# Value projections computed by rows of time, another order of the projection pairs, and a reworked first pass in an f32 hybrid encoder block

## The chip, the cores and the metric

The kernel runs on one core of one Trainium2 chip. Its engines each follow their own queue of instructions: TensorE (PE in the profile; PEld is its weight load) multiplies matrices, VectorE (DVE), ScalarE (ACT) and GpSimd (POOL) work on tiles in on-chip memory, and SyncE (SP) issues the transfers between device memory and on-chip memory. Matmuls write to PSUM, all other tiles are in SBUF. The metric is the device time of one execution in microseconds.

## The reference, cut to what matters

One encoder block on `x` of 2048 rows of time by 1024 columns, all in float32. One wide projection feeds everything else:

```python
h = rms_norm(x, norm_pre_g)
proj = jnp.einsum('bsd,de->bse', h, w_in)
u_a, z_a, q, k, v, o, z_b, gates, g_a, g_b = jnp.split(proj, split_points, axis=-1)   # 1024 columns each, gates 16
# branch A: centred window means of u_a, mixed per group, times silu(z_a)
# branch B: q, k = silu(centred depthwise conv); 4 heads of 256, chunks of 128 rows, both directions:
kw = kc * jnp.exp(w_end - m_chunk[..., None])[..., None]
c_chunk = jnp.einsum('bhcld,bhcle->bhcde', kw, vc)          # added to a running state, chunk after chunk
num = jnp.einsum('bhcls,bhcsd->bhcld', scores, vc) + inter_scale[..., None] * num_inter
# hb = sum of the directions, normalised per head; y_b = hb * sigmoid(o) * silu(z_b)
merged = jax.nn.sigmoid(g_a + b_merge[0]) * (y_a @ w_proj_pool) + jax.nn.sigmoid(g_b + b_merge[1]) * (y_b @ w_proj_mlstm)
return x + rms_norm(merged @ w_out, norm_post_g)
```

The values `v` are used with time on the rows of a matmul's operands (`kw` transposed times `vc`), while q and k are first convolved along time.

## The kernel before

**Arithmetic.** Every f32 product is made of three matmuls in a reduced-precision form of f32 (fp32r in the rows): each operand is split into an upper part (a rounded copy) and a lower part (what the copy lost), and upper x upper, upper x lower and lower x upper are added in PSUM. A split is one copy, mostly on ScalarE (L98), and one subtraction on VectorE or GpSimd (L102). Names that end in `h` and `l` are the two parts.

**Projections.** The first two thirds of the program are the projections. They run over two halves of the sequence of 1024 rows each, and in each half over 36 *pairs* of column blocks of the weights (128 columns each). `in_pairs` lists them: the merge gates `ga` and `gb` of head 0 first, then *heavy* pairs (q, k, u), each followed by some *light* ones (v, z, o with zb, and other gates), then three gate pairs. For each half, one level of the Strassen-Winograd scheme is used: the 1024 rows are two blocks of 512, the 1024 inputs two of 512, the pair's two column blocks are the third factor. `operands` makes the seven left operands from the normalised, transposed input (A11, A12, A22, S1 to S4), `prep_w` the seven right ones from the pair's weights (B11, B21, B22, T1 to T4; tiles named `wB` and `wT`). The seven products go into three accumulators `bankA`, `bankB`, `bankC`, each with two buffers in PSUM (`strassen`). One product is 4 slices x 3 terms = 12 matmuls of 512 columns, with a 128x128 weight block as the stationary operand and 512 rows of time as the moving one. So results have output columns on partitions and time along the free axis. The first two pairs of a half, `ga` and `gb` of head 0, are done without Strassen (`quarters`, L500 to L502), as their operands are ready sooner. In the first half the split weights are kept in device memory (`keep_w`) and half of them are read back in the second (`again_w`).

**Value pairs.** `pair_v` collects the four result quadrants in two tiles `raw` (L685: VectorE adds the last term while it reads PSUM). Then TensorE turns them, 128x128 at a time, against an identity matrix (`vtr`, L744), eight transposes for each block of 512 rows; the turned values are split to `vnh` and `vnl` and stored. These tiles carry two more columns, ones and zeros, which VectorE sets by memset as soon as the tile is free (L737). There are four value pairs (one per head) and two halves.

**First pass.** In the first half, before the loop of pairs, `operands` fetches the transposed input (`xT`), sums its squares (`ssqp`, L258), spreads the row factors by a matmul with the identity (`rbp`, L183), scales, and makes the combinations; two products `busy` (L281), whose result nothing reads, stand between these. `combos` splits S1 and S3 with their lower parts on GpSimd and S2 with its lower part on VectorE. The last input tiles live in rooms that the weight tiles (`wc`, 10 buffers) take over later. `gates` makes the 16 gate pre-activations beside the first pairs and copies them out of PSUM as `gsb` (L671). `fold` (L373, L379) multiplies the pooled branch's mixing and projection matrices together, piecewise between pairs at the places listed in `FOLDS`.

**Recurrence.** After the projections, `mlstm` walks over heads and chunks. Backward first: `back1` turns a chunk's keys (`kt`, L1311, two transposes of 128x128 each) and weighs them (`keys`), `back2` multiplies them with the values (`update`: `cu`, L1040 to L1042, two tiles of 128x258) and adds to the running state `cb` on VectorE (L1256), 15 states per head and direction. For head 0 backward, `keys` has a branch of its own: ScalarE writes the weighed key to a tile from the pool `w1`, VectorE copies the upper part (L1268), GpSimd subtracts. For all others ScalarE writes the upper part at once and VectorE makes the lower one (L1245). After the recurrence come the two merged branches (`branch_a`, `branch_b`) and the output projection. In the second half of the projections, weights that these later stages need are split ahead (`split_ahead`, 16 steps, one per pair from pair 12 on, `PRE`).

**What sets the order.** The program is written as generators of small steps; a tile scheduler puts each engine's instructions in order by the order of writing, by priorities (`tc.high_priority`: the weights of the next pair are prepared ahead) and by ties (`tc.issue_after(x)`: not before x in the order). All transfers of tiles are issued by SyncE. The weights of pair 2 are tied behind the last scaled input (`self.scaled[8]`), those of pair 3 are not tied.

The main loop after the two first pairs does, for each pair: prepare the weights, first product steps, the rest of the pair before, own middle steps:

```python
this, self.read_banks = work(i, W), []
next(this)
...
next(this)
run(rest)
...
next(this)
rest = this
```

The functions follow as the kernel before has them.

## Time and profile before

| | |
|---|---|
| runs of the kernel before | 2341.11, 2343.8, 2347.96 us; median 2343.8 us |
| profiled execution | 2344.1 us, span from first to last instruction 2342.3 us |
| mean granted TensorE clock | 0.993 |
| TensorE busy | 2285.9 us, 98% of the span, 11545 matmul records |
| VectorE, ScalarE, GpSimd busy | 1412.6 us (60%), 885.8 us (38%), 1184.2 us (51%) |
| transfers | 564.43 MB, mean 241 GB/s |

All rows are of one profiled execution. A group row names line, engine, operation and tiles (output <- inputs), the tile's partitions x elements and the count, then busy time, the mean of one, and the idle time just before such instructions with what ended most of it. A row of a timeline begins with the time from the span's start, then the time that the row covers, engine, line and what it is; `x4` says that four like ones are in the row, and brackets at the end give a wait and what ended it. A row of stretches gives, for each window, its length and then the busy time of TensorE, of its weight load, of VectorE, ScalarE and GpSimd, the granted clock, the busy share of the DMA engines and GB/s. Matmuls overlap in the pipeline, so a matmul's own duration (0.39 us for 512 columns) is longer than the distance from one start to the next.

### The profile page before, as it was taken

The numbers are of one execution on the slowest core, as the hardware profiler recorded it, in microseconds if no ns is written. First come the engines' busy times: TensorE is split into PE (matmuls) and PEld (weight loads), VectorE is DVE, ScalarE is ACT, GpSimd is POOL, SyncE is SP. The second block draws the span as 40 slices with busy tenths as digits, with TensorE's granted clock in tenths as the row PEclk, the third lists the DMA queues.
The fourth block names the chain that finished last, engine by engine and source line by source line (L and its number), as shares of the span: only waits on it lengthen the run. The fifth ranks groups of instructions, "written<-read, shape, count | busy, mean of one in ns | idle before, by whom it ended". The sixth has DMA issues, their size and how long they took to land. (4 is left out here: it accounts for less than half of the span.)

```text
span 2342.3 us, 32965 instructions
## 1 busy us (share of the span) xinstructions
PE 2285.9 (98%) x11545; PEld 1938.1 (83%) x11545; DVE 1412.6 (60%) x2379; ACT 885.8 (38%) x1796; POOL 1184.2 (51%) x917
## 2 busy tenths in 40 slices
PE   7899999999999999999999999899999999999998
PEld 5788888888888788888878788699998888999886
DVE  6665656768765555546656565388887453454365
ACT  5334333333343423323333233467766221111342
POOL 4755545666664533356564555245556341233574
PEclk9999999999999999999999999899999999999999
DMA  5567766766685366788888787767767696677863
GB/s 211 188 237 271 259 222 223 265 234 219 222 296 206 110 203 212 228 297 279 295 298 287 265 299 270 258 193 246 238 190 243 219 321 227 214 277 256 329 207 126
DMA packets 233270, 564.43 MB, mean 241 GB/s; under 512 B 23568, under 2 KB 70800, under 8 KB 233104
## 3 DMA queue, kind: packets, MB, share of 16 engines
q1 hardware_dynamic: 233104, 562.33, 69.7%
q8 instruction: 91, 1.49, 0.3%
q14 instruction: 75, 0.61, 0.1%
HBM read 340.46 MB, written 221.77 MB: 240 GB/s over the span
## 5 line engine op out<-in xcount | busy, mean ns | idle before, releaser
L102 POOL TENSOR_TENSOR wB<-wraw,wB 128x512 fp32r<-128x512 f32 x220 | 333.1, 1518 | 293.3 <-ACT wB L98 232.7
L98 ACT ACTIVATE wB<-wraw 128x512 fp32r<-128x512 f32 x224 | 139.3, 626 | 268.7 <-PE bankB L112 121.9
L102 POOL TENSOR_TENSOR wT<-wt,wT 128x512 fp32r<-128x512 f32 x102 | 148.5, 1459 | 128.2 <-ACT wT L98 105.5
L718 DVE SCALAR_TENSOR_TENSOR acc<-raw,conv_w,acc 128x1026 f32<-128x1026 f32 (+1 forms) x96 | 151.2, 1587 | 10.5 <-ACT acc L713 9.7
L1040 PE MATMUL pb<-oxs,w_proj_mlstm 128*128 128x256 f32 x512 | 143.9, 281 | 0.7 <-DVE sga L1206 0.4
L1042 PE MATMUL pb<-oxs,w_proj_mlstm 128*128 128x256 f32 x512 | 143.9, 281 | 0.0
L1041 PE MATMUL pb<-oxs,w_proj_mlstm 128*128 128x256 f32 x512 | 143.8, 281 | 0.0
L98 ACT ACTIVATE wT<-wt 128x512 fp32r<-128x512 f32 x136 | 85.3, 629 | 153.5 <-PE bankB L112 60.4
L1385 POOL TENSOR_TENSOR qs<-q,isc 128x256 f32<-128x256 f32 x120 | 90.0, 754 | 93.1 <-PE num L1401 59.9
L110 PE MATMUL bankB<-S3h,wT 128*128 128x512 f32 x272 | 106.2, 390 | 3.6 <-DVE u L469 3.6
L110 PE MATMUL bankB<-A22h,wT 128*128 128x512 f32 x272 | 106.1, 390 | 2.1 <-DVE u L474 2.1
L110 PE MATMUL bankA<-A12h,wB 128*128 128x512 f32 x272 | 108.0, 397 | 0.0
L110 PE MATMUL bankC<-S4h,wB 128*128 128x512 f32 x272 | 106.2, 391 | 1.2 <-DVE raw L685 1.2
L112 PE MATMUL bankA<-A11h,wB 128*128 128x512 f32 x272 | 106.0, 390 | 1.3 <-POOL wB L102 1.3
L1025 POOL TENSOR_TENSOR nm<-nm,mask 128x256 f32<-128x256 f32 x64 | 60.4, 955 | 91.4 <-DMA nm<-negM 74.2
L111 PE MATMUL bankB<-S2l,wT 128*128 128x512 f32 x272 | 106.5, 392 | 0.0
L110 PE MATMUL bankC<-S1h,wT 128*128 128x512 f32 x272 | 106.4, 391 | 0.0
L111 PE MATMUL bankC<-S4l,wB 128*128 128x512 f32 x272 | 106.4, 391 | 0.0
L112 PE MATMUL bankA<-A12h,wB 128*128 128x512 f32 x272 | 106.2, 391 | 0.0
L110 PE MATMUL bankA<-A11h,wB 128*128 128x512 f32 x272 | 106.2, 390 | 0.0
L111 PE MATMUL bankA<-A12l,wB 128*128 128x512 f32 x272 | 106.1, 390 | 0.0
L112 PE MATMUL bankC<-S4h,wB 128*128 128x512 f32 x272 | 106.1, 390 | 0.0
(417 smaller groups left out, 7097.3 us busy)
## 6 DMA issues: line engine op xcount, KB each, us to landing
wt<-wT SPq DMA_DIRECT2D x136, 512.0 KB, 4.4
wT<-wt SPq DMA_DIRECT2D x136, 512.0 KB, 6.0
wraw<-in_w_in SPq DMA_DIRECT2D x98, 512.0 KB, 5.2
vh<-vnh SPq DMA_DIRECT2D x16, 516.0 KB, 4.4
vl<-vnl SPq DMA_DIRECT2D x16, 516.0 KB, 5.7
v<-vh SPq DMA_DIRECT2D x16, 516.0 KB, 8.8
v<-vl SPq DMA_DIRECT2D x16, 516.0 KB, 8.5
xT<-in_xT SPq DMA_DIRECT2D x16, 512.0 KB, 6.5
```

The lines of the kernel that those rows point to most:

```text
L98: self.upper = nc.scalar.activation(hi, x, AF.Copy)
L102: return eng.tensor_tensor(lo, x, hi.bitcast(F32), op=ALU.subtract)
L110: nc.tensor.matmul(ps, wh, xh, start=start and kt == 0, stop=False, skip_group_check=True)
L111: nc.tensor.matmul(ps, wh, xl, start=False, stop=False, skip_group_check=True)
L112: end = nc.tensor.matmul(ps, wl, xh, start=False, stop=stop and kt == 3, skip_group_check=True)
L718: nc.vector.scalar_tensor_tensor(acc[:, :n], raw[:, tap : tap + n], self.cw[:, ct, tap : tap + 1], acc[:, :n], op0=ALU.mult, op1=ALU.add,)
L1025: nc.gpsimd.tensor_tensor(t[:, d, :, :], t[:, d, :, :], mask[:, d, None, :].to_broadcast([P, 2, P]), op=ALU.add)
L1040: nc.tensor.matmul(ps, wh, xh, start=i == 0, stop=False)
L1041: nc.tensor.matmul(ps, wh, xl, start=False, stop=False)
L1042: nc.tensor.matmul(ps, wl, xh, start=False, stop=i == n)
L1385: nc.gpsimd.tensor_tensor(qs[d], q[:, :, ck], isc[:, d, j % 2, None, :].to_broadcast([P, 2, P]), op=ALU.mult)
```

## The change

**Values by rows.** `pair_v` no longer collects and turns. Two value pairs are done together by a new function `by_rows`: the stationary operand is now 128 rows of time of an A or S operand, the moving one 256 columns of the weights of the two pairs together, so that the results have time on partitions. The weights of the value pairs are laid out for it (`columns` in `layouts`, `in_pairs`): two neighbouring value pairs now hold the columns of two heads (0 and 2, then 1 and 3), the one pair for the first half of each input block's slices, the other for the second. A product is 48 matmuls of 256 columns for the two pairs (2 pairs' input slices x 2 x 4 time blocks x 3 terms); there are 14 such products for each half. Each accumulator's two buffers belong to the same two pairs. Splits read the results directly (those of the first quadrant from PSUM, the others from SBUF), the memset of the extra columns is tied behind the split, and the first of the two pairs only runs what is left of the pair before.

**Order of the pairs.** The first two value pairs follow q of head 0, the other two follow q of head 1 (loop places 3, 4 and 8, 9); the other light pairs are spread anew. The 16 steps of `split_ahead` stand at the places listed in `PRE` in place of 12 to 27, and one place of `FOLDS` changes from 9 to 10.

**First pass.** In the first half S1's lower parts are made on VectorE. The tile of input slices 2 and 3 of the second block is now in a `raw` room, that of slices 4 and 5 in a `wc` room. The first `busy` product is tied behind the last `ssqp`, and two stand behind `rbp` where there was one. The weights of pair 3 are tied behind the last copy of the first pairs' evacuation (`self.evac`) and behind `gsb` (`self.gated`).

**Keys.** The branch of `keys` for head 0 backward is gone; these keys go the way of all others, with its two buffers.

```diff
-PRE = 12
-FOLDS = (2, 5, 7, 9, 12, 14, 16, 18)
+PRE = (4, 5, 7, 9, 10, 16, 17, 19, 20, 22, 24, 25, 27, 29, 32, 33)
+FOLDS = (2, 5, 7, 10, 12, 14, 16, 18)
...
+        c = base["v"] + h // 2 * DH
+        one["v", h] = ("v", (h // 2, h % 2), c, c + 2 * DH)
...
-    light = [("v", 0), ("o", 0), ("o", 1), ("v", 1), ("o", 2), ("v", 2), ("o", 3), ("o", 4), ("z", 0), ("o", 5)]
-    light += [("z", 1), ("v", 3), ("o", 6), ("z", 2), ("o", 7)]
+    light = [[("v", 0), ("v", 1)], [("o", 0)], [("v", 2), ("v", 3)], [("o", 1)], [("o", 2)], [("o", 3), ("z", 0)]]
+    light += [[("o", 4), ("z", 1)], [("o", 5)], [("o", 6), ("z", 2)], [("o", 7)], [edge[5], ("z", 3)], edge[6:]]
...
-        self.put(H, "S1", j, s1, "act", "pool")
+        self.put(H, "S1", j, s1, "act", le)
...
-        for b, q, where in ((0, 0, "raw"), (0, 2, "acc"), (0, 1, "acc"), (0, 3, "acc"), (1, 0, "raw"), (1, 2, "raw"), (1, 1, wc), (1, 3, wc)):
+        for b, q, where in ((0, 0, "raw"), (0, 2, "acc"), (0, 1, "acc"), (0, 3, "acc"), (1, 0, "raw"), (1, 1, "raw"), (1, 2, wc), (1, 3, wc)):
...
-            busy(X[7][0][:, :P], X[7][0])
+            with tc.issue_after(done.ins):
+                busy(X[7][0][:, :P], X[7][0])
...
-            busy(self.rstd[:, :1].to_broadcast([P, P]), X[7][0])
+            for _ in range(2):
+                busy(self.rstd[:, :1].to_broadcast([P, P]), X[7][0])
...
-        ends = [self.combos(H, j, X[j][0], X[4 + j][0], X[j][1], X[4 + j][1]) for j in range(4)]
+        ends = [self.combos(H, j, X[j][0], X[4 + j][0], X[j][1], X[4 + j][1], ("dve", "pool")[half]) for j in range(4)]
...
-                            with tc.issue_after(self.scaled[8].ins) if i == 2 else ExitStack():
+                            ties = [self.scaled[8]] if i == 2 else [self.evac, self.gated] if i == 3 else []
+                            with ExitStack() as behind:
+                                for t in ties:
+                                    behind.enter_context(tc.issue_after(t.ins))
                                 self.prep_w(W, load(i), wc, wt)
...
-                    if half == 1 and PRE <= i < PRE + 2 * KT:
+                    if half == 1 and i in PRE:
...
+                    if self.pairs[i][0] == "v":
+
+                        if self.pairs[i][1][1] == 0:
+                            first = W
+                            run(rest)
+                        else:
+                            run(work(i, (first, W)))
+                        rest = iter(())
+                        if half == 0 and i + 1 in FOLDS:
+                            next(fold)
+                        continue
...
-                        nc.tensor.transpose(ps[:, c, i * P : (i + 1) * P], t[i][:, tt : tt + P], self.ident)
-                cc = slice(c2 * 2, c2 * 2 + 2)
-                self.split(hi[:, cc, :DH], lo[:, cc, :DH], ps, "act", "dve")
...
+    def by_rows(self, H, W, psum, pool, out):
...
+        def prod(k, h, w, start):
+            for t in range(2):
+                wh, wl = (x.rearrange("p (k a) n -> p k (a n)", k=2) for x in W[t][w])
+                for tt in range(4):
+                    ps = bank[k, tt // 2][:, tt % 2, :]
+                    for j in range(2):
+                        hh, hl = (x[:, 2 * t + j, tt * P : (tt + 1) * P] for x in H[h])
+                        opens, end = start and t + j + tt % 2 == 0, t + j == 2
+
+                        with self.tc.issue_after(opened.ins) if start and not opens else ExitStack():
+                            one = nc.tensor.matmul(ps, hh, wh[:, j], start=opens, stop=False, skip_group_check=True)
+                        if opens:
+                            opened = one
+                        nc.tensor.matmul(ps, hh, wl[:, j], start=False, stop=False, skip_group_check=True)
+                        self.third = nc.tensor.matmul(ps, hl, wh[:, j], start=False, stop=end, skip_group_check=True)
...
+        prod("A", "A11", "B11", True)
+        p1 = copy("A")
+        prod("B", "S2", "T2", True)
+        u2 = plus("B", p1)
+        yield
+        prod("C", "S1", "T1", True)
+        prod("B", "S3", "T3", False)
+        u3 = plus("B", p1)
+        yield
+        give(3, "C", u3)
+        prod("A", "A12", "B21", False)
+        give(0, "A", None)
+        yield
+        prod("B", "A22", "T4", False)
+        give(2, "B", p1)
+        prod("C", "S4", "B22", False)
+        give(1, "C", u2)
...
-                if d == 1 and h == 0:
-
-                    kw = self.w1.tile([P, 2, 512], F32, tag="w", name=self.nm("kw"))[:, 0, :DH]
-                    k = self.w1.tile([P, 2, 512], F32R, tag="w", name=self.nm("k"))
-                    out = k[:, 0, :DH], k[:, 1, :DH]
-                    up = nc.scalar.activation(kw, kn[h, c // 4][:, c % 4, :], AF.Copy, scale=col["w"][:, ix(d, h, c)])
-                    nc.vector.tensor_copy(out[0], kw)
-                    nc.gpsimd.tensor_tensor(out[1], kw, out[0].bitcast(F32), op=ALU.subtract)
...
                 out = split2(io, [P, DH], f"k{d}", bufs=KB)
-                weigh(out, kn[h, c // 4][:, c % 4, :], col["w"][:, ix(d, h, c)])
+                up = weigh(out, kn[h, c // 4][:, c % 4, :], col["w"][:, ix(d, h, c)])
```

Three places where the order of an engine's instructions changes. Line numbers of the change are those of the changed file.

**ScalarE at the end of the first block.** `sg` is the sigmoid of the first two pairs' merge gates, `gsb` the copy of the gate pre-activations, `wB` and `wT` are upper parts of weights: the first two of pair 2, the others of pair 3. Before:

```order
L98 ACTIVATE wT_94_850<-wt_848 128x512
L98 ACTIVATE wB_95_853<-wraw_825 128x512
L841 ACTIVATE sg_781<-bankC_636,b_merge 128x512
L98 ACTIVATE wB_110_956<-wraw_952 128x512
L841 ACTIVATE sg_784<-bankC_637,b_merge 128x512
L98 ACTIVATE wT_113_963<-wt_961 128x512
L841 ACTIVATE sg_793<-bankA_644,b_merge 128x512
L98 ACTIVATE wT_114_966<-wt_959 128x512
L841 ACTIVATE sg_796<-bankB_645,b_merge 128x512
L671 ACTIVATE gsb_801<-gps_688 32x512
L98 ACTIVATE wT_116_971<-wt_969 128x512
```

After:

```order
L101 ACTIVATE wT_95_852<-wt_850 128x512
L101 ACTIVATE wB_96_855<-wraw_827 128x512
L930 ACTIVATE sg_783<-bankC_638,b_merge 128x512
L930 ACTIVATE sg_786<-bankC_639,b_merge 128x512
L930 ACTIVATE sg_795<-bankA_646,b_merge 128x512
L930 ACTIVATE sg_798<-bankB_647,b_merge 128x512
L692 ACTIVATE gsb_803<-gps_690 32x512
L101 ACTIVATE wB_111_958<-wraw_954 128x512
L101 ACTIVATE wT_114_965<-wt_963 128x512
L101 ACTIVATE wT_115_968<-wt_961 128x512
L101 ACTIVATE wT_117_973<-wt_971 128x512
```

The three splits for pair 3 that stood between the sigmoids now stand behind `gsb`.

**TensorE in the first value work of the first half.** `bankB` is the accumulator of the second of the seven products' chains, `vtr` the PSUM tile that takes the transposes, `raw` the collected results. Before:

```order
L112 MATMUL bankB_1141<-S3h_414,wT_138_1120 128x512
L744 MATMUL vtr_1227<-ident,raw_989 128x128
L744 MATMUL vtr_1227<-ident,raw_990 128x128
...
L744 MATMUL vtr_1234<-ident,raw_989 128x128
L744 MATMUL vtr_1234<-ident,raw_990 128x128
...
L110 MATMUL bankA_1140<-A12h_408,wB_139_1123 128x512
L111 MATMUL bankA_1140<-A12l_409,wB_139_1123 128x512
```

After, at the step from the first pair's input slices to the second's within the product S2 x T2:

```order
L773 MATMUL bankB_1070<-wT_114_965,S2h_412 128x256
L776 MATMUL bankB_1070<-wT_114_965,S2h_412 128x256
L777 MATMUL bankB_1070<-wT_114_965,S2l_413 128x256
L773 MATMUL bankB_1069<-wT_128_1041,S2h_412 128x256
L776 MATMUL bankB_1069<-wT_128_1041,S2h_412 128x256
L777 MATMUL bankB_1069<-wT_128_1041,S2l_413 128x256
```

No transposes are left; the weights stream past as the 256-column operand, first those loaded as one pair (`wT_114`), then those of the other (`wT_128`), into both buffers of the bank.

**TensorE where the recurrence begins.** `kt` is the turned key block, `cu` the chunk's update of the state. Before, 17 rows of `kt` stand between the last projection and the first `cu`; here are the last five:

```order
L1311 MATMUL kt_12082<-ident,kT_11992 128x128 x2
L1311 MATMUL kt_12106<-ident,kT_11992 128x128 x2
L1311 MATMUL kt_12126<-ident,kT_11992 128x128 x2
L1311 MATMUL kt_12146<-ident,kT_11992 128x128 x2
L1311 MATMUL kt_12164<-ident,kT_12079 128x128 x2
L1040 MATMUL cu_11853<-v_1720_11825,k_11839 128x258
L1041 MATMUL cu_11853<-v_1721_11826,k_11839 128x258
L1040 MATMUL cu_11858<-v_1720_11825,k_11839 128x258
```

After, from the last matmul of the projections on:

```order
L115 MATMUL bankC_12135<-S4h_6853,wB_1663_12130 128x512
L1392 MATMUL kt_12324<-ident,kT_12311 128x128 x2
L1392 MATMUL kt_12332<-ident,kT_12311 128x128 x2
L1392 MATMUL kt_12351<-ident,kT_12311 128x128 x2
L1392 MATMUL kt_12370<-ident,kT_12311 128x128 x2
L1129 MATMUL cu_12341<-v_1673_12315,k_1679_12328 128x258
L1130 MATMUL cu_12341<-v_1674_12316,k_1679_12328 128x258
L1129 MATMUL cu_12346<-v_1673_12315,k_1679_12328 128x258
```

Four key blocks now stand ahead of the first update; the others are interleaved with the updates behind it.

More of the change, by code (lines that the diff above doesn't have):

```diff
@@ L257, in sums @@
             for i in range(4):
[L258 to L259 removed]
+                done = nc.tensor.matmul(
+                    ps[:, i : i + 1], acc[:, i * P : (i + 1) * P], self.one_c, start=True, stop=True
+                )
+            with tc.issue_after(done.ins):
+                busy(X[7][0][:, :P], X[7][0])
             ssq = pool.tile([P, 4], F32, tag="ssq", name=self.nm("ssq"), bufs=2)
@@ L1247, in weigh @@
                 )
+                return up
             def update(new, kw, v, old, keep):
```

93 lines of the change are left out of this document (62 added, 31 removed).

## Prediction, before the changed kernel was run

> **What bounds the kernel now.** I read the engine shares first, then busy time by stretches, then the timelines around the stretches in which TensorE is not full.
>
> ```profile
> PE 2285.9 (98%) x11545; PEld 1938.1 (83%) x11545; DVE 1412.6 (60%) x2379; ACT 885.8 (38%) x1796; POOL 1184.2 (51%) x917
> ...
> 60.00:120.00 60.00, 53.09 (x225) 42.31 (x224) 37.81 (x44) 22.29 (x41) 44.23 (x27) 0.94 0.53 192
> 300.00:360.00 60.00, 60.00 (x275) 50.15 (x275) 32.18 (x45) 20.98 (x40) 29.60 (x20) 1.00 0.65 226
> 1200.00:1260.00 60.00, 54.17 (x239) 44.21 (x238) 40.62 (x47) 16.89 (x26) 31.45 (x23) 0.97 0.85 292
> 1500.00:1560.00 60.00, 51.80 (x333) 47.64 (x334) 44.59 (x141) 36.79 (x101) 29.91 (x40) 0.86 0.69 235
> 2040.00:2100.00 60.00, 60.00 (x510) 60.00 (x510) 32.27 (x56) 11.16 (x18) 16.66 (x19) 1.00 0.81 282
> ```
>
> TensorE bounds the program: full in ordinary stretches (300 to 360), short by 6.9 us in the row from 60 to 120, 5.8 us around 1230, 8.2 us around 1530. So a change pays in two ways only: fewer or shorter TensorE instructions, or fewer holes. In 2040 to 2100, where only 256-column products of the merge stage run, 510 starts fit in 60 us: 117.6 ns each.
>
> **Values by rows: the TensorE work.** In the projection stage a 512-column matmul starts every 226.5 ns:
>
> ```profile
> 299.82 0.39 PE L110 MATMUL bankC<-S1h,wT 128*128 128x512 f32 x1
> ...
> 305.03 0.40 PE L112 MATMUL bankB<-S3h,wT 128*128 128x512 f32 x1
> ...
> 305.27 1.03 PE L744 MATMUL vtr<-ident,raw 128*128 128x128 f32 x8
> ...
> 306.37 0.39 PE L111 MATMUL bankA<-A12l,wB 128*128 128x512 f32 x1
> ...
> L744 PE MATMUL vtr<-ident,raw 128*128 128x128 f32 x128 | 18.0, 282 | 5.0 <-DVE raw L685 5.0
> ...
> 1516.88 0.28 PE L1040 MATMUL cu<-v,k 128*128 128x258 f32 x1
> ...
> 1517.86 0.28 PE L1042 MATMUL cu<-v,k 128*128 128x258 f32 x1
> ```
>
> From 299.82 to 305.03 are 23 intervals: 5.21 / 23 = 226.5 ns. Between the first transpose (305.27) and the second matmul behind the eight (306.37) lie 1.10 us, of which one 512-column interval is 0.23: eight transposes take 0.87 us, 109 ns each. All 128 go: -14.0 us.
>
> In their place: each value pair has 84 matmuls of 512 columns per half (7 products, 4 slices, 3 terms); 4 pairs and 2 halves make 672. By rows the moving side is the weights of two pairs, 256 columns: 4 groups of 7 x 48 = 336, so 1344. The columns streamed are the same; the price is the fixed part of a matmul, paid twice. At 117.6 ns: 158.1 against 672 x 226.5 ns = 152.2 us, +5.9. The projection stage shows no 256-column fp32r matmul, so both ends: half a 512-column one (113.25 ns) gives 0; the 258-column rows above (8 intervals in 0.98 us, 122.5 ns, or 121.6 for 256) give +11.2. I take 117.6: same width, 1536 cases. **Term: -8.1 us, from -14.0 to -2.8.**
>
> The Trainium skill (TensorE: Matmul & The Clock Gate, "Back-to-back issue gap") has a warm gap of N/2.4 + 2.5 ns: 109.2 ns at 256 columns and 215.8 at 512. By it doubling the count would cost 1.7 us, and the sum would be 4.2 us lower. The trace disagrees at both widths (226.5 and 117.6), and I go by the trace.
>
> The evacuations hardly change: ten adds of 128x512 and eight splits per two pairs as before, and two ScalarE copies fewer. The products last 48 x 117.6 = 5.6 us each, where a pair's took 12 x 226.5 = 2.7, so VectorE has twice as long for each bank; against that both buffers of every bank belong to one group. I cost this at nothing, covered by those 5.6 us; if the cover fails, see the fourth rival.
>
> **The wait that the transposes made.**
>
> ```profile
> 1223.99 0.07 DVE L737 MEMSET vnh<- 128x8 f32 x1 [0.99 <-DMA kT<-acc]
> ...
> 1229.39 0.68 DVE L685 TENSOR_TENSOR raw<-bankC,u 128x512 f32<-128x512 f32 x1 [1.55 <-issue]
> ...
> 1230.13 1.76 PE L744 MATMUL vtr<-ident,raw 128*128 128x128 f32 x7 [3.93 <-DVE raw L685]
> ...
> 1232.11 0.63 PE L111 MATMUL bankA<-A12l,wB 128*128 128x512 f32 x1
> ```
>
> VectorE stands in the memset of a value tile until an older tile has been stored; the adds behind it come late, and TensorE waits 3.93 us in front of the transposes and then runs slow (0.63 us a matmul instead of 0.39). The change has neither transposes nor that memset ahead (it follows the split), and moves the last value pairs from the heavy stretch to before the first pooled pair. The hole is some 6.6 us: 0.7 before 1223, 3.93, some 2 of slow clock. What is late next is the same adds for other pairs, so I count two thirds: **-4.5 us, from -7 to 0.**
>
> **First block.**
>
> ```profile
> 54.32 14.99 POOL L102 TENSOR_TENSOR S1l<-xT,S1h 128x512 fp32r<-128x512 f32 x4 [3.71 <-ACT S1h L98]
> 69.27 5.95 POOL L102 TENSOR_TENSOR S3l<-xT,S3h 128x512 fp32r<-128x512 f32 x4
> ...
> 69.34 0.63 ACT L98 ACTIVATE wB<-wraw 128x512 fp32r<-128x512 f32 x1 [9.07 <-POOL S1l L102]
> ...
> 70.53 1.84 DVE L102 TENSOR_TENSOR S2l<-xT,S2h 128x512 fp32r<-128x512 f32 x1 [6.11 <-ACT S2h L98]
> ...
> 76.50 0.50 PE L112 MATMUL bankA<-A11h,wB 128*128 128x512 f32 x1 [1.34 <-POOL wB L102]
> ...
> 81.64 1.89 PE L373 MATMUL fps<-fm,fw 128*128 128x256 f32 x8
> 89.11 3.78 PE L373 MATMUL fps<-fm,fw 128*128 128x256 f32 x8 [5.57 <-ACT gsb L671]
> ...
> 88.48 0.57 ACT L671 ACTIVATE gsb<-gps 32x512 f32<-32x512 f32 x1
> ```
>
> The four S1 lower parts hold POOL until 69.3. Pair 2's first weight split waits for them (9.07 us of ScalarE, since the weight tile takes an input tile's place), its lower part queues behind S3 as well, and TensorE waits 1.34. Later the folding product needs a PSUM tile that gsb reads; gsb stands on ScalarE behind splits for pair 3 and ends at 89.05, 5.5 us after the first fold's end (83.53). After that wait eight fold matmuls take 3.78 us instead of 1.89: 1.9 of slow clock.
>
> The change gives S1's lower parts to VectorE, lets only S1 inputs stand where weight tiles come next, and puts pair 3's preparation behind the sigmoids and gsb. Four VectorE splits cost 2.8 us at 0.69 (7.1 at the 1.77 shown below), inside the 6.11 us that VectorE idles there. ScalarE gets back more than the 5.5 us by which gsb is late. Pair 3 is held back by some microseconds, and TensorE wants it only a pair later. The holes sum to 1.34 + 5.57 + 1.9 = 8.8; I take **-8.5, from -9.4 to 0.**
>
> **Start.**
>
> ```profile
> 11.76 1.87 PE L258 MATMUL ssqp<-one_c,sq 128*128 128x1 f32 x8 [0.36 <-DVE sq L254]
> 15.37 2.08 PE L183 MATMUL rbp<-ident,rstd 128*128 128x128 f32 x8 [1.74 <-POOL rstd L161]
> 17.24 1.91 PE L281 MATMUL busy<-xT,rstd 128*128 128x512 f32 x2
> 20.43 0.79 PE L500 MATMUL bankA<-A11h,wB 128*128 128x512 f32 x1 [1.27 <-ACT A11h L98]
> ...
> 24.43 0.63 PE L502 MATMUL bankB<-A11l,wB 128*128 128x512 f32 x1
> ...
> 25.13 0.39 PE L502 MATMUL bankB<-A11l,wB 128*128 128x512 f32 x1
> ```
>
> The 11 intervals from 20.43 to 25.13 take 4.70 us, at full clock 2.5: 2.2 lost. The idle product moves into the gap at 13.6 to 15.4, and a second one stands at 19.15. If TensorE is warm at 20.4, 2.2 are won; the second product, 1.9 long, ends at 21.06 and delays the first real one by 0.6. **-1.6, from -2.2 to +0.6.**
>
> **First blocks of the recurrence.**
>
> ```profile
> 1492.23 0.60 PE L1311 MATMUL kt<-ident,kT 128*128 128x128 f32 x4
> ...
> 1505.78 0.66 PE L1311 MATMUL kt<-ident,kT 128*128 128x128 f32 x2 [2.30 <-DMA kT<-kT]
> 1508.23 0.58 PE L1040 MATMUL cu<-v,k 128*128 128x258 f32 x1 [1.79 <-DVE k L1268]
> ...
> 1504.53 0.88 DVE L1245 SCALAR_TENSOR_TENSOR k<-kn,col_w,k 128x256 fp32r<-128x256 f32 x2 [11.41 <-ACT k L1244]
> 1507.89 1.24 DVE L1268 CAST k<-kw 128x256 fp32r<-128x256 f32 x2
> ...
> 1527.06 4.47 DVE L1256 SCALAR_TENSOR_TENSOR cb<-cb,col_keep,cu 128x258 f32<-128x258 f32 x11
> ```
>
> Today 17 transposed key blocks stand on TensorE ahead of the first state update, the last of them waiting for the next head's keys; the first update starts at 1508.23, 16 us after the first transpose, and the 15 states are done at 1531.5. The order of the change has the first update behind four blocks, at about 1496.5. Then a key costs VectorE 0.44 + 2 x 0.41 = 1.26 us; 15 take 18.9 at least, 23.3 if they go as slowly as now, plus some 4 us for the first chunk's scores, which now stand behind: 1519.4 to 1523.8, so 8 to 12 earlier. Two key buffers in place of the four that the old branch had can slow the chain; at 2.0 us a key it ends at 1530.5. Between 12 and, with the chain slower still, -2: **-6.5, from -12 to +2.**
>
> **Order and split-ahead.** The pairs are the same ones, and the 16 split-aheads the same instructions; spread over pairs that follow light ones they meet less work, covered by VectorE's idle 40% (32 to 41 of 60 us busy above). 0, from -3 to +3.
>
> **Sum.** -8.1 - 4.5 - 8.5 - 1.6 - 6.5 = -29.2 on the profiled execution's own 2344.1 us (span 2342.3): 2314.9. It stands 0.3 above the median of the runs, 2343.8, so **2315 us**.
>
> **Rivals.**
> 1. More is won (2304): the 256-column matmul costs half a 512-column one (-5.9) and the recurrence starts 12 earlier (-5.5). For it: weight loads are the limit at 117.6 ns (PEld full in that row), and pairs of matmuls share a weight here.
> 2. The first block and the recurrence do not do what they are for: S1 on VectorE contends with S3 on POOL, ScalarE still waits, and the two key buffers eat the earlier start. Only values and start remain with half of the wait: 2344.1 - 8.1 - 1.6 - 2 = 2332. For it: four S1 splits took 14.99 us on POOL while VectorE was busy, against 5.95 for four S3 behind them.
> 3. Port contention: 24 of the 32 value splits now read their input from SBUF, not PSUM.
>
> ```profile
> 79.36 1.74 POOL L102 TENSOR_TENSOR wB<-wraw,wB 128x512 fp32r<-128x512 f32 x1
> ...
> 79.87 1.77 DVE L426 TENSOR_TENSOR wt<-wraw,wt 128x512 f32<-128x512 f32 x1
> ...
> 94.18 0.69 DVE L426 TENSOR_TENSOR wt<-wraw,wt 128x512 f32<-128x512 f32 x1 [2.19 <-DMA wraw<-in_w_in]
> ```
>
> The same VectorE subtraction takes 1.77 us beside a POOL split and 0.69 without: 24 x 1.08 = 26 us, which if all of it reached TensorE gives 2341, no change. Against it: 5.6 us of cover per product. The Trainium skill (SBUF — State Buffer, "Who interferes with whom") says that a VectorE instruction with two SBUF inputs contends with a GpSimd one that reads SBUF; these rows agree.
> 4. Slower: a value group owns both buffers of each bank, so each reuse waits for VectorE: four within a group, three on entry, three on exit, 40 in all. Two adds need 1.4 us of 5.6, so it decides where VectorE is over 4.2 us late. At 1 us each: 2315 + 40 = 2355. The profile has VectorE that late once, around 1230.
>
> **Numbers.** Forecast 0.54 (2307 to 2324), rival 1 0.13, rival 2 0.17, rival 3 0.09, rival 4 0.07. What a measurement tells from no change is 0.3%, 7 us. Faster: 0.54 + 0.13 + 0.17 + 0.01 of rival 3 = 0.85; within 0.3%: 0.08; slower: 0.07. Range 2303 to 2334: it takes in rivals 1 and 2 and leaves out 0.16.
>
> **What would show it.** No vtr rows, and value matmuls starting every 113 to 122 ns, with no gap over 1 us on TensorE in the four groups; a gap before bank B or C ended by VectorE speaks for rivals 3 or 4. The fold's second half directly behind the first, no wait for gsb, first real matmuls at 0.39 us. The first state update near 1497 less what was won before it. If the projection stage ends less than 15 us earlier, the first block or the value price was wrong; if the recurrence's first state chain ends over 23 us behind the last projection, the sixth term was.

## The result, and the profile after

The changed kernel takes 2319.7 us (median of 5 runs, 2318.2 to 2324.1) where the kernel before takes 2345.05 (5 runs, 2341.1 to 2348.0): a ratio of 0.9893, 95% interval 0.9878 to 0.9907, 25.3 us less. The forecast was 2315, with a range of 2303 to 2334.

The shares of busy time, and the busy time by stretches (length; TensorE, its weight load, VectorE, ScalarE, GpSimd; granted clock, DMA share, GB/s). The first three windows are those of the prediction; the fourth begins 20 us earlier than there, because the recurrence now begins 10.9 us earlier:

```profile
PE 2273.6 (98%) x12091; PEld 1955.6 (84%) x12091; DVE 1434.1 (62%) x2383; ACT 883.6 (38%) x1788; POOL 1165.6 (50%) x898
...
60.00:120.00 60.00, 54.55 (x304) 47.16 (x303) 38.95 (x42) 24.07 (x44) 42.02 (x25) 0.94 0.55 201
300.00:360.00 60.00, 60.00 (x267) 50.00 (x266) 34.75 (x44) 19.77 (x37) 34.28 (x24) 1.00 0.63 224
1200.00:1260.00 60.00, 51.46 (x217) 41.79 (x217) 37.22 (x42) 14.91 (x23) 33.11 (x22) 0.91 0.71 239
1480.00:1540.00 60.00, 57.56 (x390) 51.79 (x389) 49.88 (x148) 43.88 (x123) 21.93 (x29) 1.00 0.88 311
```

Only one of the three stretches that were short has become full: the beginning of the recurrence (57.6 of 60 us at full clock; before, 51.8 at 0.86). 60 to 120 is nearly as it was, and 1200 to 1260 has lost more than before (51.5 in place of 54.2).

The same by stages, each boundary read from the starts in TensorE's own rows (first product of the projections; last gate product of the first block; first `bankB` product of the second half; last projection; first product of the second merged branch; end):

| stage | before, us | after, us | difference |
|---|---|---|---|
| up to the first product | 20.43 | 20.06 | -0.4 |
| first two pairs | 53.87 | 51.77 | -2.1 |
| rest of the first half | 691.71 | 685.74 | -6.0 |
| second half | 725.99 | 723.59 | -2.4 |
| recurrence, pooled branch | 501.85 | 488.21 | -13.6 |
| second merged branch, output | 348.47 | 352.97 | +4.5 |

That is 20.0 us in these two traces. The last stage has the same instructions in the fourteen traces of this study (but for the order of some sums in the last kernel) and takes 347.9 to 355.8 us in them. The profiled execution of the changed kernel was the longest of its five, so the stages ahead of the last, 24.5 us together, are nearer to the medians' 25.3.

What TensorE waited for in the projections behind the first block (total us, times, longest), before:

```profile
PE fps L373 <- ACT gsb L671: 5.6, 1, 5.6
PE vtr L744 <- DVE raw L685: 5.0, 3, 3.9
PE bankB L110 <- DVE u L469: 3.6, 3, 1.7
PE bankB L110 <- DVE u L474: 2.1, 2, 1.3
PE bankA L112 <- POOL wB L102: 1.3, 1, 1.3
PE bankC L110 <- DVE raw L685: 1.2, 1, 1.2
```

and after:

```profile
PE bankB L113 <- DVE u L481: 10.1, 3, 8.2
PE bankB L113 <- DVE u L476: 5.4, 1, 5.4
PE bankB L773 <- DVE u L788: 0.9, 1, 0.9
PE bankB L113 <- DVE raw L706: 0.4, 1, 0.4
```

The three waits that the change removed (`gsb`, `vtr`, `wB`: 11.9 us) are gone by name. Their time is not: 18.8 us have become 16.8. Nearly all of it now ends with VectorE's two first sums of a bank (`u`, L476 and L481).

### The profile page after: what moved, and what is told of

It reads as the page before. It is cut to its first block, busy times and chain, and to the rows that moved or that the text cites. A ratio compares the mean times of both kernels' runs of the same rounds, so it can differ in the third digit from the quotient of the medians.

```text
span 2322.3 us, 34037 instructions
## 1 busy us (share of the span) xinstructions
PE 2273.6 (98%) x12091; PEld 1955.6 (84%) x12091; DVE 1434.1 (62%) x2383; ACT 883.6 (38%) x1788; POOL 1165.6 (50%) x898
## 4 chain that ended last, share of the span: by engine, by line
PE 35%; DMA 7%; DVE 4%; issue 2%; POOL 2%; ACT 2%; SPq 1%; POOLq 0%; DVEq 0%; ACTq 0%
PE num L1482 4%; PE pb L1129 2%; PE pb L1130 2%; PE pb L1131 2%; PE paps L1130 2%; PE paps L1131 2%; PE paps L1129 2%; PE bankB L113 2%; PE bankB L115 2%; PE bankB L114 2%; PE cu L1129 1%; DMA ox<-mg 1%; PE cu L1130 1%; PE bankC L114 1%; PE bankC L115 1%
## 5 line engine op out<-in xcount | busy, mean ns | idle before, releaser
L113 PE MATMUL bankB<-A22h,wT 128*128 128x512 f32 x240 | 94.6, 394 | 10.1 <-DVE u L481 10.1
L433 DVE TENSOR_TENSOR wt<-wraw,wt 128x512 f32<-128x512 f32 x68 | 63.4, 932 | 64.2 <-POOL wT L105 45.5
L1129 PE MATMUL paps<-pys,w_proj_pool 128*128 128x512 f32 x256 | 101.0, 395 | 0.0
L1130 PE MATMUL paps<-xa,w_proj_pool 128*128 128x512 f32 x256 | 100.8, 394 | 0.1
L1131 PE MATMUL paps<-pys,w_proj_pool 128*128 128x512 f32 x256 | 100.7, 394 | 0.0
L1615 POOL TENSOR_TENSOR pa<-pa,sgb 128x256 f32<-128x256 f32 x64 | 48.6, 773 | 102.9 <-DVE sgb L1614 66.2
L113 PE MATMUL bankB<-S3h,wT 128*128 128x512 f32 x240 | 94.4, 393 | 5.4 <-DVE u L476 5.4
L476 DVE TENSOR_TENSOR u<-bankB,p 128x512 f32<-128x512 f32 x68 | 46.6, 686 | 83.8 <-PE bankB L115 82.9
L1129 PEld LDWEIGHTS pb<-oxs,w_proj_mlstm 128*128 128x128 f32 x512 | 96.4, 188 | 2.2 <-issue 1.4
L1131 PEld LDWEIGHTS pb<-oxs,w_proj_mlstm 128*128 128x128 f32 x512 | 96.7, 189 | 0.0
L1130 PEld LDWEIGHTS pb<-oxs,w_proj_mlstm 128*128 128x128 f32 x512 | 96.4, 188 | 0.0
L113 PE MATMUL bankA<-A12h,wB 128*128 128x512 f32 x240 | 94.3, 393 | 0.0
```

Source lines behind the costliest of these rows:

```text
L113: nc.tensor.matmul(ps, wh, xh, start=start and kt == 0, stop=False, skip_group_check=True)
L433: nc.vector.tensor_tensor(t, x, y, op=ALU.subtract)
L1129: nc.tensor.matmul(ps, wh, xh, start=i == 0, stop=False)
L1130: nc.tensor.matmul(ps, wh, xl, start=False, stop=False)
L1131: nc.tensor.matmul(ps, wl, xh, start=False, stop=i == n)
```

## Experiments

Each of the first kernels undoes one part of the change; the others repair what the traces showed. Times are medians. Each ratio is taken to runs of the kernel before on the same chip; their median was 2344.9 us beside the kernels with the old keys, the old values, the whole old first pass and the old places of the split-ahead steps, 2342.1 beside the changed kernel run once more and the three kernels with one repair, and 2343.3 beside the other four.

**The keys of head 0 backward as before.**

```diff
+                if d == 1 and h == 0:
+                    kw = self.w1.tile([P, 2, 512], F32, tag="w", name=self.nm("kw"))[:, 0, :DH]
+                    k = self.w1.tile([P, 2, 512], F32R, tag="w", name=self.nm("k"))
...
```

> The changed kernel with one part undone: the keys of head 0 backward are again made by their own branch (ScalarE, then VectorE, then GpSimd, in tiles of w1). Theory: this branch alone put 17 key blocks ahead of the first state update. Then the first update comes again some 16 us behind the first key transposes (2.6 us in the changed kernel), the first states are done some 39 us behind the last projection (25 us), and the time is 2319.7 + 13.7 = 2333 us (2330 to 2336). Rival: the early start comes from the values, which the new order of the pairs stores earlier; then the first update stays within 5 us of the first key transposes and the time within 3 us of 2320.

Measured: 2333.0 us (4 runs, 2330.4 to 2334.3), ratio to before 0.9951 (0.9934 to 0.9967). The stage of the recurrence takes 501.4 us, 13.2 more than in the changed kernel; before it was 501.9. The branch alone did it, as the theory had it: with it 17 key blocks stand ahead of the first update again, without it four. TensorE and VectorE in this kernel, where the recurrence begins:

```profile
1493.17 0.66 PE L1400 MATMUL kt<-ident,kT 128*128 128x128 f32 x2 [2.31 <-DMA kT<-kT]
1495.64 0.58 PE L1129 MATMUL cu<-v,k 128*128 128x258 f32 x1 [1.81 <-DVE k L1357]
...
1496.24 0.42 PE L1129 MATMUL cu<-v,k 128*128 128x258 f32 x1
...
1491.91 0.88 DVE L1334 SCALAR_TENSOR_TENSOR k<-kn,col_w,k 128x256 fp32r<-128x256 f32 x2 [11.38 <-ACT k L1333]
```

and in the changed kernel:

```profile
1481.38 0.60 PE L1392 MATMUL kt<-ident,kT 128*128 128x128 f32 x4
1483.36 0.71 PE L1392 MATMUL kt<-ident,kT 128*128 128x128 f32 x4 [1.37 <-ACT kn L1395]
1484.03 0.39 PE L1129 MATMUL cu<-v,k 128*128 128x258 f32 x1
...
1504.35 1.05 PE L1455 MATMUL s<-q,kT 128*128 128x128 f32 x8
...
1502.61 0.88 DVE L1346 SCALAR_TENSOR_TENSOR cb<-cb,col_keep,cu 128x258 f32<-128x258 f32 x2
```

With the branch, the first update comes 16.0 us behind the first key transposes (1479.64) and runs on a slow clock (0.42 us a product). Without it, it comes 2.65 us behind them at full clock, and VectorE's last sum of the 15 backward states ends at 1503.5: 19.5 us behind the first update, 1.30 us a state. The first chunk's scores (`s`) follow only then.

**The value pairs as before.**

```diff
-        yield from self.by_rows(H, W, psum, pool, out)
+        t = yield from self.collect(H, W, psum, pool, HALF, 0)
+        ...
+                        nc.tensor.transpose(ps[:, c, i * P : (i + 1) * P], t[i][:, tt : tt + P], self.ident)
```

> The changed kernel with the value pairs done as before (collect, 128 transposes, memset ahead of the split), at the same places in the order of the pairs. Theory of the price: 128 transposes at 109 ns come back (+14.0 us) and 1344 products at 120 ns (161.3 us) become 672 at 226.5 ns (152.2 us), so 2319.7 + 4.9 = 2324.6 us. Rival 1: the memset and the transposes also bring back a wait of TensorE as at 1222 to 1233 before; then 2329 to 2332. Rival 2: by-rows values cost elsewhere (VectorE's sums from SBUF, both buffers of a bank) what they save on TensorE; then 2320 or less.

Measured: 2328.7 us (2326.8 to 2330.0), ratio 0.993 (0.9915 to 0.9945): 9.0 more than the changed kernel, between the price (4.9) and the first rival (9.3 to 12.3). The first half is 5.3 us longer and the second 4.0. The price is measured in the changed kernel, where one product of 48 matmuls begins at 107.85 and the next at 113.61:

```profile
107.85 0.28 PE L773 MATMUL bankB<-wT,S2h 128*128 128x256 f32 x1
...
113.61 0.28 PE L773 MATMUL bankC<-wT,S1h 128*128 128x256 f32 x1
```

5.76 / 48 = 120.0 ns, the same in the six products of this group that run without others between them. So 1344 take 161.3 us, 9.1 more than the 672 before, and the values alone win 14.0 - 9.1 = 4.9. The other 4 us are in part waits in this kernel, whose table reads

```profile
PE bankB L110 <- DVE u L478: 9.1, 3, 6.3
PE bankB L110 <- DVE u L473: 8.8, 3, 5.4
PE bankC L110 <- DVE raw L692: 0.7, 1, 0.7
```

That is 18.6 us, 1.8 more than in the changed kernel, and one of these waits, of 2.0 us at 229, has some 3.6 us of slow clock behind it. No wait is for `vtr`: the transposes are back, the wait in front of them is not. So it did not come from the transposes and their memset alone; it went with the old order of the pairs and its list of split-ahead steps.

**The whole first pass as before.**

```diff
-            for _ in range(2):
+            for _ in range(1):
...
-        ends = [self.combos(..., ("dve", "pool")[half]) for j in range(4)]
+        ends = [self.combos(..., "pool") for j in range(4)]
...
-                            ties = [self.scaled[8]] if i == 2 else [self.evac, self.gated] if i == 3 else []
+                            ties = [self.scaled[8]] if i == 2 else []
```

> The changed kernel with the first pass undone: S1's lower parts on GpSimd, the old rooms, one idle product behind the row factors, pair 3 not tied. Theory: what the changed kernel had won when pair 2's third bank product began is lost (2.5 us of start and 2.1 us in the first block): 2319.7 + 4.5 = 2324 us, with waits of TensorE of 1.3 and some 5.5 us between 74 and 92 us. Rival: what is won there is taken back by later waits, so 2320 us; or the first block is worth the 8.5 us of the prediction, 2330 us.

Measured: 2325.4 us (2322.1 to 2327.7), ratio 0.9916 (0.9898 to 0.9933). The waits came back as expected, but in the trace the second merged branch begins at 1970.0, only 0.6 us later than in the changed kernel; the rest of this profiled execution's difference lies in the last stage (355.8 us, the longest of all). The next two kernels take the part apart.

**Only the idle products as before; only the rest of the first pass as before.** Their edits are the first, and the other two, of the diff above, with the idle product put ahead of the sums of squares again, and the old rooms.

> The changed kernel with only the idle products of the first pass as before: the first ahead of the sums of squares, one instead of two behind the row factors. Theory from the traces: with these old products the first real matmuls ran slowly in the trace of before (2.2 us lost) and at full speed in the trace of the kernel with the whole old first pass (the matmul that follows them began at 19.4 us there, 20.1 to 20.4 in the changed kernel), so this part wins or loses up to 2 us by chance: 2318 to 2321 us. Rival: it is what makes the whole old first pass 5.7 us slower in its median; then 2324 us.

> The changed kernel with only the rest of the first pass undone: S1's lower parts on GpSimd, the old rooms, pair 3 not tied; the idle products as changed. Theory from the traces: TensorE's waits in the first block come back as they were (1.3 us at 75, 5.6 us at 84 in place of 5.5 us at 84), so some 1 to 2 us are lost, 2320 to 2321 us. Rival: this part is what makes the whole old first pass 5.7 us slower; then 2324 us.

Measured: 2318.6 us (2318.0 to 2323.5) and 2321.75 (2320.7 to 2322.6); the changed kernel took 2319.7 in the result and 2318.4 when it was run once more. Both are near their theories, and neither part reaches the 2324 of the rivals. The parts together come to some 1 to 3.5 us, which the traces bear out: the first two pairs take 53.2 us with the old idle products (51.8 with the new), and the rest of the first half 688.5 us with the old block (685.7 and 686.6 in two traces of the changed kernel). The 5.7 us of the whole are not accounted for by its parts. In the trace of the whole the rest of the first half takes 686.95 us, hardly more than in the changed kernel. With four runs each, and a last stage that varies by up to 8 us, the difference may be chance; it stays open.

What the idle products do was not the same in every trace. TensorE's first products in the kernel with the whole old first pass, in the one with the old idle products alone, and in the changed kernel:

```profile
19.39 0.50 PE L504 MATMUL bankA<-A11h,wB 128*128 128x512 f32 x1 [0.43 <-ACT A11h L101]
19.73 0.39 PE L505 MATMUL bankA<-A11h,wB 128*128 128x512 f32 x1
```

```profile
20.17 0.79 PE L506 MATMUL bankA<-A11h,wB 128*128 128x512 f32 x1 [1.27 <-ACT A11h L101]
20.76 0.63 PE L507 MATMUL bankA<-A11h,wB 128*128 128x512 f32 x1
```

```profile
20.06 0.50 PE L507 MATMUL bankA<-A11h,wB 128*128 128x512 f32 x1 [0.68 <-ACT A11h L101]
20.39 0.39 PE L508 MATMUL bankA<-A11h,wB 128*128 128x512 f32 x1
```

With the same old products the start was slow in two of three traces (that of before among them: 53.9 us for the first two pairs) and at full clock in one (51.8); with the new ones it was at full clock in all eleven (51.8). The Trainium skill (TensorE: Matmul & The Clock Gate, Part 1) says that the window by which the clock is granted runs freely, so that the number of slow matmuls at a kernel's start differs from run to run; that fits the two outcomes with the same old products. But the three traces do not show that it was chance alone: the fast one also has the shortest wait in front of the first product, 0.43 us, where the two slow ones have 1.27. With the new products starts behind waits of up to 1.44 us were at full clock.

**The split-ahead steps at pairs 12 to 27 again.**

```diff
-PRE = (4, 5, 7, 9, 10, 16, 17, 19, 20, 22, 24, 25, 27, 29, 32, 33)
+PRE = tuple(range(12, 28))
```

> The changed kernel with the 16 split-ahead steps at the pairs 12 to 27 again. Theory: TensorE's hole of 9.0 us at 1237 (and 2.0 us of slow clock behind it) is made by the split-ahead step of pair 24, whose second tile waits for the store of a mask tile, with two mask tiles made in that pair; places 12, 15, 18, 21, 24 and 27 are such pairs too, 24 among them, so the hole stays or comes at another of them: 2316 to 2324 us. Rival: only what precedes pair 24 in the new list makes it; then the hole is gone and the time is some 2309 us.

Measured: 2328.6 us (2326.0 to 2334.0), ratio 0.9933 (0.9913 to 0.9953). Both numbers were wrong. The hole at 1237 is smaller, but there are many more; TensorE's waits between 1060 and 1340 us in this kernel:

```profile
PE bankB L113 <- DVE u L476: 7.7, 7, 2.4
PE bankB L113 <- DVE u L481: 4.8, 4, 3.9
```

(In the changed kernel there are two in that stretch, 8.2 and 0.4 us.) The second half takes 732.2 us, 8.6 more than in the changed kernel and 6.2 more than before, though its values are 2.4 us cheaper. So with the old list the new order of the pairs costs some 8.6 us, and the new list gets them back: the two together are worth nothing, as forecast, but as a loss and a gain. The 8.6 us are a difference of stages less the price of the values; the old order with values by rows was not run.

**Pair 3's weights tied behind pair 2's first sum.** In the changed kernel the wait in the first block had moved from the fold to the S3 product. Its TensorE, ScalarE and VectorE there:

```profile
77.52 3.62 PE L380 MATMUL fps<-fm,fw 128*128 128x256 f32 x16
...
89.35 0.79 PE L113 MATMUL bankB<-S3h,wT 128*128 128x512 f32 x1 [5.45 <-DVE u L476]
...
90.37 0.63 PE L115 MATMUL bankB<-S3h,wT 128*128 128x512 f32 x1
...
82.76 1.67 ACT L101 ACTIVATE wT<-wt 128x512 fp32r<-128x512 f32 x3 [3.54 <-DVE wt L433]
84.34 0.58 ACT L470 ACTIVATE p<-bankA 128x512 f32<-128x512 f32 x1
...
87.06 1.64 DVE L433 TENSOR_TENSOR wt<-wraw 128x512 f32<-128x512 f32 x1
88.62 0.68 DVE L476 TENSOR_TENSOR u<-bankB,p 128x512 f32<-128x512 f32 x1
```

The fold's 16 products now stand together, without a wait. But pair 2's copy of bank A, ready since 74.96, stands behind three splits for pair 3 that wait for VectorE, and its first sum behind differences for pair 3.

```diff
-                            ties = ... [self.evac, self.gated] if i == 3 else []
+                            ties = ... [self.evac, self.gated, self.read_banks[0]] if i == 3 else []
```

> The changed kernel with pair 3's weights tied behind pair 2's first sum on VectorE as well. Theory: in the changed kernel the wait in front of the S3 product at 83.9 us (5.45 us and 1.8 of slow clock behind it) comes from pair 3's splits and differences standing ahead of pair 2's copy of bank A on ScalarE and of its first sum on VectorE. Then it goes, the second merged branch begins 6 to 7 us earlier (1962 to 1964), and the time is 2313 us. Rival: pair 3's weights come late in their turn and TensorE waits as long in front of the first value product; then nothing is won, 2320 us.

Measured: 2312.3 us (2310.2 to 2313.9), ratio 0.9872 (0.9857 to 0.9887), where the changed kernel on the same chip took 2318.4. The copy now comes at 78.20, the sum at 80.52, and the S3 product starts without a wait:

```profile
78.20 0.57 ACT L470 ACTIVATE p<-bankA 128x512 f32<-128x512 f32 x1
...
80.52 0.68 DVE L476 TENSOR_TENSOR u<-bankB,p 128x512 f32<-128x512 f32 x1
...
82.82 0.39 PE L113 MATMUL bankB<-S3h,wT 128*128 128x512 f32 x1
```

The rest of the first half falls from 685.7 to 679.9 us, and the second merged branch begins at 1959.9, earlier than forecast. From the last gate product to the A12 product of pair 2 TensorE took 24.1 us before and 22.1 in the changed kernel; here it takes 14.6. A wait of 1.57 us for the second sum follows at 91.5. The cause is shown.

**The changed kernel once more.**

> The changed kernel itself once more, for a second trace beside the others. In the traces so far the stretch from the first product of the second merged branch to the last product took 340.0 us before, 344.4 in the changed kernel and 339.3 to 347.3 in its variants, all with the same instructions there. Theory: that stretch varies by itself, and up to its start (1969.4 us) the kernel repeats within 1 us; time 2318 to 2324. Rival: the changed kernel is slower in that stretch; then it is 344 us again, and never under 342.

Measured: 2318.4 us (2314.7 to 2322.5), ratio 0.9899 (0.9881 to 0.9918). The second merged branch begins at 1970.8 (1969.4 in the first trace), and the last stage takes 349.9 us: that stage varies by itself, as the theory had it. Up to its start the kernel repeated within 1.4 us, not 1. Half of that is in the first block: behind the same wait of 5.4 us the slow clock lasted 3.6 us in the first trace and some 5.7 in this one. Here and in the kernels with the old first pass the hole near 1240 is 5.4 to 8.2 us long.

**The hole near 1240.** In the changed kernel SyncE stores a mask tile at 1227.69, and ScalarE, VectorE and TensorE go on as follows:

```profile
1227.69 0.48 SPq L1117 DMA_DIRECT2D nm<-nm  x1
...
1236.22 0.63 ACT L101 ACTIVATE wp<-wp 128x512 fp32r<-128x512 f32 x1 [13.51 <-DMA wT<-wt]
...
1236.89 0.69 DVE L105 TENSOR_TENSOR wp<-wp,wp 128x512 fp32r<-128x512 f32 x1 [10.52 <-ACT wp L101]
...
1248.67 0.68 DVE L481 TENSOR_TENSOR u<-bankB,p 128x512 f32<-128x512 f32 x1
...
1249.40 0.80 PE L113 MATMUL bankB<-A22h,wT 128*128 128x512 f32 x1 [8.15 <-DVE u L481]
```

By the trace's record of the transfer the mask's store landed at 1236.04, the split started 0.18 us later. (The row names another transfer as what ended the wait; that it was the mask's store is inferred from the two times.) VectorE stands 10.5 us in front of that split's lower part, then does pooled window sums, and the sum `u` comes at 1248.67. Two ways round it: other pairs, or the split ahead of the masks.

```diff
-PRE = (4, 5, 7, 9, 10, 16, 17, 19, 20, 22, 24, 25, 27, 29, 32, 33)
+PRE = (4, 5, 7, 9, 10, 16, 17, 19, 20, 22, 25, 26, 28, 29, 31, 32)
```

> The changed kernel with the split-ahead steps of pairs 24, 27 and 33 at 26, 28 and 31, so that none stands in a pair that makes two mask tiles and comes after them. Theory: TensorE's hole at 1237 (9.0 us and 2.0 of slow clock) is ScalarE standing in the split of pair 24's step, whose second tile waits for the store of the first of two mask tiles (landed at 1236.04, the split starts at 1236.22). Then the hole goes and the time is 2309 to 2311 us. Rival: the transfers around pair 24 are late whatever stands there, so another wait of 4 to 9 us takes its place; 2316 to 2320 us.

Measured: 2314.1 us (2312.2 to 2316.0), ratio 0.988 (0.9866 to 0.9895). The second half falls by 5.7 us, half of what the theory had: that wait is gone, but others of 2.29 and 1.59 us, each for a first sum, end at 1251.85 and 1369.60. The first of them also brings a slow clock:

```profile
1251.85 0.50 PE L113 MATMUL bankB<-S3h,wT 128*128 128x512 f32 x1 [2.29 <-DVE u L476]
...
1252.42 0.63 PE L115 MATMUL bankB<-S3h,wT 128*128 128x512 f32 x1
...
1255.83 0.40 PE L114 MATMUL bankB<-S3l,wT 128*128 128x512 f32 x1
```

```diff
-                            for u in range(...): self.masked(u, mask)
-                    if half == 1 and i in PRE: ... self.split_ahead(...)
+                    if half == 1 and i in PRE: ... self.split_ahead(...)
+                            for u in range(...): self.masked(u, mask)
```

> The changed kernel with the split-ahead step written ahead of the mask tiles of the same pair, in the list of the changed kernel. By the same theory the split's tile waits for a store of the pair before, which has landed long ago; the hole at 1237 goes, and the mask tiles wait in its place, on GpSimd, where a wait of some us costs TensorE nothing: 2309 to 2312 us. Rival: GpSimd's wait holds up the lower parts of weights queued behind the masks, and TensorE waits there: 2316 us or more.

Measured: 2320.6 us (2318.6 to 2322.8), ratio 0.9905 (0.9889 to 0.9922), the same as the changed kernel. The wait near 1242 shrank to 3.0 us and one of 2.4 came at 1317. The hole shrank, as the theory had it, but that does not pay: sums that were late by the one thing are late by the next. Whether GpSimd is what made them late, as the rival says, was not followed up.

**Both repairs, and both with the sums put ahead.**

> The changed kernel with both repairs: pair 3's weights tied behind pair 2's first sum, and the split-ahead steps of pairs 24, 27 and 33 at 26, 28 and 31. Alone they gave 6.2 and 4.4 us against the changed kernel on the same chip. Theory: they lie 1100 us apart and add up: 2318.4 - 10.6 = 2308 us. Rival: the wait near 1240 follows the place of the transfers, which shift with the first repair, and comes back; then 2312 us.

Measured: 2309.5 us (2309.4 to 2309.8), ratio 0.9854 (0.9837 to 0.987): faster than both kernels, 33.8 us less than the kernel before on the same chip. Taken as times the repairs add up to 8.9 of the 10.6 us; the changed kernel was not run on this chip, and by the ratios (0.9854 against its 0.9899) it is 10.5. What is left of TensorE's waits in the projections behind the first block:

```profile
PE bankB L113 <- DVE u L476: 3.9, 3, 2.2
PE bankB L113 <- DVE u L481: 3.2, 3, 1.6
PE bankB L773 <- DVE u L788: 0.2, 1, 0.2
```

```diff
+        with self.tc.high_priority(offset=300):
             nc.scalar.activation(p1, bank["A"], AF.Copy)
...
+        with self.tc.high_priority(offset=300):
             self.read_banks.append(nc.vector.tensor_tensor(u2, bank["B"], p1, op=ALU.add))
```

> The kernel with both repairs, and besides the copy of bank A and the two first sums of every pair without by-rows are put ahead in the order of ScalarE and VectorE. Theory: the waits that are left in the projections (1.1 us at 832, some 4 at 1249, 1 to 2 at 1223, 1368 and 1476) are all ended by such a sum that stood behind window sums or split-ahead work, so 4 to 7 us more are won: 2302 to 2304 us. Rival: the sums wait for TensorE or for the copy anyway, so what is put behind them is late in its turn; 2306 to 2310 us.

Measured: 2310.6 us (2308.6 to 2313.1), ratio 0.9859 (0.9844 to 0.9874). Nothing is won, as the rival said, 0.6 us above its range. TensorE's waits for such sums are 8.0 us in all here, 7.3 without: put ahead in the order they were not earlier, which fits the rival's reason but was not traced further.

## Why the prediction was right, and where it was not

The direction, the size (25.3 us of 28.8) and the range were right. That the sum came out so near is in part luck: misses of both signs cancelled. The terms as measured below come to some 23 us.

- **Values, -8.1 forecast.** The transposes are gone. The price per 256-column product was 120.0 ns, not 117.6, inside the stated bounds (113.25 to 121.6): -4.9. The merge stage's own distance is nearer 118 (the middle of all its rows) than the 117.6 of one stretch; why products of the same width differ by 2 ns between two stages no run here shows. That VectorE covers the evacuations was right: one short wait of 0.9 us in the value groups (`u` L788), so rivals 3 and 4 fell.
- **The wait in front of the transposes, -4.5.** Wrong: 0. It is gone by name, but the same stretch then had a longer one (8.2 us and 2 of slow clock near 1240), which moving a split-ahead step takes away in the main. The prediction said that the same adds would be late next and still counted two thirds; the second half as a whole shows only the values' own 2.4 us.
- **First block, -8.5.** Wrong in size: about -2, by the traces up to pair 2's A12 product (24.1 us before, 21.8 to 22.8 in the traces of the changed kernel and of those kernels that keep its first block); undoing it cost 1.9 to 2.8 in one trace and 0.3 to 1.2 in another. The prediction's own sign says the same: the projections ended 10.9 us earlier, less than the 15 that it set. The `wB` and `gsb` waits went as described. The step that failed is the sentence that pair 3 "is held back by some microseconds, and TensorE wants it only a pair later": pair 3's preparation, tied behind `gsb`, still stood ahead of pair 2's own copy and sum, and TensorE waited 5.45 us for those. One more tie won the 6 us and brought this stretch to 9.5 us less than before: the holes were priced about rightly, the order behind `gsb` was not foreseen.
- **Start, -1.6.** About right in the profiles (-2.5), but the old products gave a fast start in one trace of three, so the size depends on which was seen; undone, it moved the median by nothing that can be told.
- **Recurrence, -6.5, from -12 to +2.** Wrong in size: -13.6, outside its own bounds. The mechanism was right and is shown by undoing it (13.2). The first update came 2.65 us behind the first transposes, not 4.3; the states took 19.5 us, near the least of the 18.9 to 23.3; the chain ended 22.3 us behind the start of the last projection product, inside the 23 that the prediction set (39.5 before). With these two figures and the 4 us for the scores the prediction's own working gives some 13. The step that failed is the halving for fear of the two key buffers: at 1.30 us a state, where VectorE's work alone is 1.26, they cost next to nothing.
- **Order and split-ahead, 0.** Right in sum, and for another reason than given: not because VectorE's idle time covers it, but because the new list wins back the 8.6 us that the new order costs.

Rivals 1 (2304) and 2 (2332) each had one half right: the recurrence won more, the first block and the wait less. The last stage's scatter of several microseconds in single traces was not foreseen.

## What to carry to other kernels

A wait that is removed by moving the instruction named in the row tends to come back at whatever stands next ahead of the same consumer; look for everything that stands ahead of the sum or copy which frees an accumulator, on each engine's queue, and tie the work for later pairs behind that. Undo the parts of a change singly: here the new order lost about 8.6 us and the new list won them back, which no single time shows. Where a stage repeats only to some microseconds, compare stages by their boundaries in the trace, not one execution's total.

## What the runs showed of the hardware that was not expected

- A 256-column fp32r product whose moving side is the weights starts every 120.0 ns, where the merge stage's ran at 117.6 (118 by the middle of all its rows).
- In these traces a GpSimd split of SBUF tiles did not get done while VectorE worked without a break on tiles in SBUF. In the changed kernel VectorE's sums and splits follow each other from before 54 to 65.57 us, at 0.68 us each; GpSimd's first S3 split begins at 54.41 and ends only at 66.71, and its next three take 1.28 us each (all four 16.04). In the kernel before the first S1 split did the same (11.24 us, the next three 1.29 each), and its four S3 splits behind it took 5.95 in all. So one split is held up, not four slowed down:

```profile
54.41 12.29 POOL L105 TENSOR_TENSOR S3l<-xT,S3h 128x512 fp32r<-128x512 f32 x1 [6.26 <-ACT S3h L101]
...
64.88 0.69 DVE L105 TENSOR_TENSOR S2l<-xT,S2h 128x512 fp32r<-128x512 f32 x1
```

  The Trainium skill (SBUF — State Buffer, "Who interferes with whom") says that only the port pair which these two engines share causes contention, and that it is an exclusive lock. A split that ends 1.1 us behind VectorE's last instruction fits that; the rows do not show the lock itself.
- A wait of TensorE in the projections costs more than itself from some two microseconds on. In the changed kernel's trace the products behind the wait of 5.45 us were slow for 3.6 us (0.79, then 0.63 in place of 0.39); after the one of 2.29 us in the kernel with moved split-ahead steps it began 0.6 us late and lasted 3.4 us. In all traces, behind the first two pairs, every wait of 2.0 us or more had such a stretch behind it except one of 2.06, and waits of 1.78 and less had none. The stretches lasted some 3 to 6 us, differently behind the same wait. At 0.43 us from start to start in place of 0.23 that loses an estimated 1 to 3 us, so the wait of 2.29 us cost about 4.
